# Two score buffers from pair 2 on, upper parts on ScalarE and remainders a unit later, in a hybrid attention layer on Trainium2

## The chip, the cores and the metric

The kernel runs on one core of one Trainium2 chip. The metric is the device time of one execution in microseconds, as the median of several runs. The engines are TensorE (PE; PEld is its weight load), VectorE (DVE), ScalarE (ACT), GpSimd (POOL) and SyncE (SP), whose queue issues nearly all transfers. Each engine works through its own instructions in order; semaphores order the engines among each other.

## The reference

One layer on 1024 tokens of width 1024, batch 1. The input is normalised, scaled and shifted, and projected to two groups of 8 heads of 64 columns: forgetting attention (a softmax with a bias from cumulated forget gates) and stick-breaking attention. Each head's output is gated by a SiLU, all are projected back, and a weighted residual is normalised again.

```python
u = _layer_norm(x) * (1.0 + scale) + shift
fq, fk, fv, fg, ff, sq, sk, sv, sg = _split_columns(u @ w_in)
f_cum = cumsum(log_sigmoid(ff + b_f))
# forgetting block: softmax over causal keys
s = q @ k.T * HEAD_DIM ** -0.5 + (f_q[:, None] - f_k[None, :])
fox = softmax(where(causal, s, -inf)) @ v
# stick-breaking block
z = q @ k.T * HEAD_DIM ** -0.5
later = reversed_cumsum(log_sigmoid(-z)) - log_sigmoid(-z)
sb = where(strict, exp(log_sigmoid(z) + later), 0.0) @ v
y = concat(fox * silu(fg), sb * silu(sg)) @ w_out
out = layer_norm(ALPHA * x + gate * y) * ln_g + ln_b
```

## The kernel before

The 16 heads are 8 pairs: pairs 0 to 3 are stick-breaking, 4 to 7 forgetting. A unit (p, h, i) is one head of one pair and one block of 128 queries against its (i + 1) * 128 causal keys, so there are 128 units. The list `units` (line 1193) goes pair by pair. In pairs 1 to 3 a head's blocks go upwards, in 4 to 6 downwards.

Matrix products are made of an upper and a lower part (`hi`, `lo`) of each operand, three products for a projection. The projections of later pairs (`gen_m` for queries, keys and gates, `gen_v` for values, `gen_split_out` for the output weights) are cut into steps and run as fillers between the units: the loop at line 1249 calls `scores_turn(k)`, `weights_turn(k)` and `fill(...)`, and `FILL` (line 1165) says how many steps a pair gets. TensorE's order is the program's; that of the other engines and of SP's queue is made by a scheduler from the dependencies, with `after(...)` to hold an instruction behind others.

What a unit does (`att_scores`, line 565):

- TensorE writes the scores to `S` (L578, L579), a tile of two PSUM banks with one buffer (line 75). The lower part of the query comes from `qz`, which ScalarE casts ahead (L525).
- In pairs 4 to 7 VectorE adds the forget bias and takes the minimum (L586); ScalarE makes the exponential and its sum (L591); VectorE makes the reciprocal and its scale (L592, L593) and adds the causal mask for the next unit (L563). POOL writes the upper float16 part of the weights (L596) and VectorE the remainder (L598) to a `room`.
- In pairs 0 to 3 ScalarE makes two sigmoids (L605, L607), VectorE a running product (L613, L617) and POOL the weights `be` (L619). From pair 2 on ScalarE writes the upper part (L626) and VectorE the remainder (L627) in the same unit.
- In pairs 0 and 1 the weights are turned by TensorE into a `T` bank (L643, two buffers) and copied by ScalarE and VectorE (L645, L646). From pair 2 on SP's queue turns them with a transposing transfer from `room` to `pt` (L551). A pair of blocks then multiplies the values (`att_pv`, L661), `LAG_CROSSED` = 4 units after the scores; ScalarE and VectorE add the two halves (L687, L688), POOL multiplies by the gate (L693), and the result goes to DRAM (L701).

Values of pairs 2 to 7 are float16 with a scale from the weights' norms. `squares` (L395) makes them from each group's split weights when that group's turn comes, on VectorE, and `range_of_v` (L398 to L408) follows before the first value tile can be evacuated. Output weights are loaded, multiplied by the gate vector, split by POOL and stored to `wo_dr` (L1019, L1020); `load_wo` brings them back in pair 7, when the tiles of `u` come free. `fetch_w` loads each weight piece to one of two staging tiles (L127), from which POOL makes the upper and lower part (L131, L132) in a ring of five.

```python
    def s_tile(name):
        return ps.tile([P, 2, 512], F32, tag="S", bufs=1, name=name)
...
            scaled[:] = [*scaled[-3:], nc.gpsimd.tensor_scalar(hi, ab, l, 1.0, op0=ALU.mult, op1=ALU.mult)]
            lows[:] = [*lows[-2:],
                       nc.vector.scalar_tensor_tensor(lo, ab, l, hi, op0=ALU.mult, op1=ALU.subtract)]
            cross(u, two)
```

Of the kernel before, what the change touches and what calls it, by code (L numbers as in the profile page):

```python
# [31 lines left out]
def tile_hybrid_layer(  # L32
# [333 lines left out]
    def range_of_u():  # L366
# [17 lines left out]
        top = t_tile("u_top")[:, 0:1]  # L384
        nc.tensor.matmul(top, ones[0:1, :].to_broadcast([1, P]), rng[0:1, 3:4], start=True, stop=True)
        nc.vector.tensor_scalar(rng[:, 4:5], top, 1.0e-30, None, op0=ALU.max)
        nc.vector.reciprocal(rng[:, 4:5], rng[:, 4:5])

    def squares(g, quarters):
        n = 528 if g == 1 else 512  # L390
        fr = rng[:, 5:9]
        for h, (hi, lo) in enumerate(quarters):
            hf = hi.bitcast(F32)[:, :n]
            sq = v_two[g].rearrange("p i t c -> p (i t c)").bitcast(BF16)[:, -n:]
            nc.vector.tensor_tensor_reduce(out=sq, in0=hf, in1=hf, op0=ALU.mult, op1=ALU.add, scale=1.0,  # L395
                                           scalar=0.0, accum_out=fr[:, h:h + 1])

    def range_of_v(g):  # L398
        fp = t_tile(f"v_range_{g}")[:, :4]
        nc.tensor.matmul(fp, ones.to_broadcast([P, P]), rng[:, 5:9], start=True, stop=True)  # L400
        up, down = (rng[:, c:c + 1] for c in (7 + 2 * g, 8 + 2 * g))
        nc.vector.tensor_reduce(out=up, in_=fp, op=ALU.add, axis=mybir.AxisListType.X)
# [124 lines left out]
    room, room_at, unsent = [], [0], []  # L527

    def two_parts(u):

        n = 2 * (u[2] + 1) * P
        if not room or u == ROOMS[len(room)]:
            room.append(sb.tile([P, 4 * SEQ], F16, tag="v", bufs=3, name=f"room_{len(room)}"))
            room_at[0] = 0
        if room_at[0] + n > 4 * SEQ:
            room_at[0] = 0
        two = room[-1][:, room_at[0]:room_at[0] + n]
        room_at[0] += n
        t4 = two.rearrange("p (b x c) -> p b x c", x=2, c=P)
        return two, t4[:, :, 0, :], t4[:, :, 1, :]  # L540
# [24 lines left out]
    def att_scores(u, following):  # L565
# [15 lines left out]
        if p >= 4:  # L581
# [3 lines left out]
            with after(*lows[:1]):  # L585
                nc.vector.tensor_tensor_reduce(out=v3(a), in0=S[:, :ns, :w], in1=v3(f),  # L586
                                               op0=ALU.add, op1=ALU.min, scale=-1.0, scalar=BIG,
                                               accum_out=nm)
# [7 lines left out]
            scaled[:] = [*scaled[-3:], nc.gpsimd.tensor_scalar(hi, ab, l, 1.0, op0=ALU.mult, op1=ALU.mult)]  # L596
            lows[:] = [*lows[-2:],
                       nc.vector.scalar_tensor_tensor(lo, ab, l, hi, op0=ALU.mult, op1=ALU.subtract)]  # L598
            cross(u, two)
        else:  # L600
# [22 lines left out]
            else:  # L623
                two, hi, lo = two_parts(u)
                bb = be[:, :ke].rearrange("p (b c) -> p b c", c=P)
                nc.scalar.activation(hi, bb, AF.Copy, scale=UP)  # L626
# [52 lines left out]
    def att_sum(acc, p, h, j):  # L679
# [20 lines left out]
        else:  # L700
            nc.sync.dma_start(y_dr[p, r, qs], yt[r, :])  # L701
# [630 lines left out]
```

## Time and profile before

| what | value |
|---|---|
| median of 3 runs | 726.84 us (726.46 to 730.42) |
| the profiled execution | 728.52 us |
| its span | 726.8 us, 10992 instructions |
| PE busy | 657.2 us (90%) |
| PEld busy | 540.3 us (74%) |
| DVE busy | 520.0 us (72%) |
| POOL busy | 434.3 us (60%) |
| ACT busy | 344.9 us (47%) |
| mean granted clock of TensorE | 0.958 |
| transferred | 109.87 MB, mean 151 GB/s |
| transposing transfers | 96, median 3.5 us to landing |

Busy time is an average over stages with different limits, so the tables by stage matter more. PEclk is the clock that TensorE was granted, 1.00 being full. A row of waits reads: engine, line, waited for; total us, times, longest us. A row of groups reads: line, engine, operation, tile written from tiles read, count; busy us, mean ns of one; idle time before them by releaser.

### The profile page before, as it was taken

The page shows a single profiled execution, that of the slowest core. Times are in us where ns is not written, and L with a number is a line of the kernel's source. Part 1 is how long each engine was busy: PE and PEld are TensorE (multiplying, and loading weights), DVE is VectorE, ACT ScalarE, POOL GpSimd, SP SyncE. Part 2 cuts the span into 40 slices and gives each one's busy share as a digit, 9 for nine tenths or more (in the row PEclk, how much of TensorE's full clock was granted, in tenths as well). Part 3 has the DMA queues.
Part 4 walks back from the last instruction along what each step waited for, and adds up shares of the span by engine and source line. Part 5 has one row for each costly group of instructions (what it writes and reads, how often), then busy time and mean ns, then how long its engine had stood idle before and what let it go on. Part 6 is the DMA issues. An engine that isn't in the chain of part 4 may idle for free.

```text
span 726.8 us, 10992 instructions
## 1 busy us (share of the span) xinstructions
PE 657.2 (90%) x3530; PEld 540.3 (74%) x3530; DVE 520.0 (72%) x1013; ACT 344.9 (47%) x753; POOL 434.3 (60%) x537
## 2 busy tenths in 40 slices
PE   8999999999999978969799788959998995799996
PEld 5798897788987766869677566749976763588785
DVE  6788689888668779975767645766777864596545
ACT  5567377656576656764634333424344542221000
POOL 6550576656385847681676777868795442675611
PEclk9999999999999999998999998978999998899999
DMA  9983331112023455452769777666786799867211
GB/s 333 398 296 118 102 72 44 41 41 63 5 66 86 100 129 118 103 141 51 204 138 185 173 190 199 166 169 179 196 216 153 161 343 275 215 168 194 95 58 59
DMA packets 160138, 109.87 MB, mean 151 GB/s; under 512 B 118928, under 2 KB 133840, under 8 KB 160080
## 3 DMA queue, kind: packets, MB, share of 16 engines
q1 hardware_dynamic: 158496, 104.70, 53.6%
q10 hardware_dynamic: 1584, 4.47, 2.3%
q8 instruction: 28, 0.46, 0.3%
q14 instruction: 30, 0.25, 0.1%
HBM read 60.34 MB, written 16.29 MB: 105 GB/s over the span
## 4 chain that ended last, share of the span: by engine, by line
PE 54%; POOL 10%; DMA 10%; issue 9%; DVE 9%; ACT 5%; SPq 1%; POOLq 0%; ACTq 0%; DVEq 0%
PE m L318 4%; DMA pt<-room 4%; PE pv L661 4%; PE m L316 4%; PE m L317 4%; PE o L1060 4%; PE o L1061 4%; PE o L1062 4%; DMA wss<-in_w_ss_dram 3%; PE S L578 3%; PE v L428 3%; PE v L430 3%; PE v L429 3%; PE S L579 3%; PE pv L672 2%
## 5 line engine op out<-in xcount | busy, mean ns | idle before, releaser
L316 PE MATMUL m<-uh,whi 128*128 128x512 f32 x304 | 124.9, 411 | 4.6 <-POOL whi L131 4.2
L318 PE MATMUL m<-uh,wlo 128*128 128x512 f32 x304 | 123.2, 405 | 4.4 <-POOL wlo L132 4.4
L317 PE MATMUL m<-ul,whi 128*128 128x512 f32 x304 | 122.1, 402 | 0.0
L619 POOL TENSOR_TENSOR be<-be,kp 128x127 f32<-128x127 f32 (+3 forms) x64 | 83.5, 1305 | 40.6 <-DVE kp L617 25.1
L598 DVE SCALAR_TENSOR_TENSOR room<-a,l,room 128x1024 f16<-128x1024 f32 (+4 forms) x64 | 70.3, 1102 | 39.9 <-POOL room L596 39.3
L578 PE MATMUL S<-k,q 128*128 128x512 f32 (+5 forms) x192 | 71.6, 374 | 18.2 <-DVE nm L586 15.3
L591 ACT ACTIVATE a<-a,nm 128x1024 f32<-128x1024 f32 (+3 forms) x64 | 49.7, 777 | 73.7 <-DVE nm L586 59.6
L596 POOL TENSOR_SCALAR room<-a,l 128x1024 f16<-128x1024 f32 (+4 forms) x64 | 53.0, 830 | 47.2 <-DMA pt<-room 15.8
L661 PE MATMUL pv<-pt,v_g 128*128 128x256 f16 x480 | 62.7, 284 | 14.0 <-DMA pt<-room 10.8
L318 PEld LDWEIGHTS m<-uh,wlo 128*128 128x128 f32 x304 | 58.7, 193 | 20.1 <-POOL wlo L132 6.1
L661 PEld LDWEIGHTS <-v_g 128*128 128x128 f16 x480 | 46.6, 105 | 33.3 <-issue 14.7
L613 DVE TENSOR_TENSOR_SCAN kp<-kp,floor 128x128 f32<-128x128 f32 (+3 forms) x64 | 58.6, 915 | 17.1 <-ACT kp L605 16.6
L316 PEld LDWEIGHTS m<-uh,whi 128*128 128x128 f32 x304 | 58.6, 193 | 16.2 <-POOL whi L131 5.5
L693 POOL TENSOR_TENSOR ty<-ty,sg 64x256 f32<-64x256 f32 x64 | 50.0, 782 | 29.1 <-DVE ty L688 19.4
L317 PEld LDWEIGHTS m<-ul,whi 128*128 128x128 f32 x304 | 58.5, 192 | 10.3
L579 PE MATMUL S<-kl,qz 128*128 128x512 f32 (+5 forms) x192 | 66.1, 346 | 0.0
L428 PE MATMUL v<-whi_v,uh 128*128 128x256 f32 (+1 forms) x192 | 57.3, 299 | 9.3 <-ACT room L626 5.4
L525 ACT CAST qz<-q 64x128 fp32r<-64x128 f32 x128 | 37.2, 295 | 51.4 <-PE S L579 50.0
L430 PE MATMUL v<-wlo_v,uh 128*128 128x256 f32 (+1 forms) x192 | 56.7, 295 | 4.0 <-POOL wlo_v L132 4.0
L578 PEld LDWEIGHTS S<-k,q 128*128 128x128 f32 x192 | 36.9, 192 | 31.2 <-DVE nm L586 21.8
L586 DVE CUSTOM_DVE_ANT_0 a<-S,fb 128x1024 f32<-128x1024 f32 (+3 forms) x64 | 48.2, 752 | 15.6 <-PE S L579 14.8
L605 ACT ACTIVATE kp<-S 128x384 f32<-128x384 f32 (+4 forms) x96 | 43.7, 491 | 32.8 <-PE S L579 31.5
(325 smaller groups left out, 1660.5 us busy)
## 6 DMA issues: line engine op xcount, KB each, us to landing
raw<-in_w_qkg_dram SPq DMA_DIRECT2D x38, 256.0 KB, 2.9
wss<-in_w_ss_dram SPq DMA_DIRECT2D x14, 512.0 KB, 8.3
x<-in_x_dram SPq DMA_DIRECT2D x8, 512.0 KB, 6.5
k<-k SPq DMA_DIRECT2D x32, 128.0 KB, 2.3
wg<-in_w_gate_dram SPq DMA_DIRECT2D x8, 512.0 KB, 4.8
raw_o<-in_w_out_dram SPq DMA_DIRECT2D x16, 256.0 KB, 3.1
fb<-f_dr ACTq DMA_DIRECT2D x8, 512.0 KB, 4.4
wo_dr<-whi_o SPq DMA_DIRECT2D x16, 256.0 KB, 2.4
```

What stands on the lines that cost most here:

```text
L316: nc.tensor.matmul(acc, hi[:, c], u_hi[kt][:, s], start=(kt == 0), stop=False)
L317: nc.tensor.matmul(acc, hi[:, c], u_lo[kt][:, s], start=False, stop=False)
L318: nc.tensor.matmul(acc, lo[:, c], u_hi[kt][:, s], start=False, stop=(kt == NB - 1))
L428: nc.tensor.matmul(acc[:, :n], u_hi[kt][:, ts_], hi[:, s], start=(kt == 0), stop=False)
L430: nc.tensor.matmul(acc[:, :n], u_hi[kt][:, ts_], lo[:, s], start=False, stop=(kt == NB - 1))
L578: nc.tensor.matmul(S[:, s, :w], qst[p][h][:, qs], kst[p][h][:, ks], start=True, stop=False)
L579: nc.tensor.matmul(S[:, s, :w], z, klo[p][:, ks], start=False, stop=True)
L596: scaled[:] = [*scaled[-3:], nc.gpsimd.tensor_scalar(hi, ab, l, 1.0, op0=ALU.mult, op1=ALU.mult)]
L598: nc.vector.scalar_tensor_tensor(lo, ab, l, hi, op0=ALU.mult, op1=ALU.subtract)]
L613: last_dve = nc.vector.tensor_tensor_scan(rv, rv, floor[:, :ke - lo], initial=0.0, op0=ALU.mult, op1=ALU.max)
L619: nc.gpsimd.tensor_tensor(be[:, :ke - 1], be[:, :ke - 1], kp[:, 1:ke], op=ALU.mult)
L661: nc.tensor.matmul(acc[:, q0:256], vt[p][:, kb, h * P:(h + 1) * P], pt[:, 2 * kb + x_, q0:], start=(kb == 0 and x_ == 0), stop=(kb == last ...
```

## The change

- From pair 2 on there are two score tiles, tags S and T. The two `T` banks, which only the first two pairs and the start use, are now one tile of two halves taken in turn, and scores alternate between it and S. The two small products of the forget rows use a score tile too, and so does the last piece of the output projection.
- In the forgetting pairs ScalarE writes the upper part instead of POOL. The remainder and the transfer of a unit are made in the next unit (`owed`, `pay`): after that unit's reduction, or in pairs 2 and 3 after its sigmoids and running product, where the upper part is moved too.
- Parts and turned weights have rooms of their own (`homes`): five fixed tiles, of which each block pair has its own stretch, while parts take the least recently used stretch. `LAG_CROSSED` is 5. Pairs 2 and 3 take their blocks from the large to the small.
- Stores of gated results and output weights are kept in a list and issued on SP's queue after a later unit's transfer.
- The norms of all value weights come from extra loads of the raw weights in pair 0, twelve loads and twelve squares, in place of `squares` and `range_of_v` in each group's turn.
- The last normalisation's gain and bias go to tiles of the query pool.

```diff
-        return ps.tile([P, 512], F32, tag="T", bufs=2, name=name)
-
-    def s_tile(name):
-        return ps.tile([P, 2, 512], F32, tag="S", bufs=1, name=name)
+        if not t_pair:
+            t_pair.append(ps.tile([P, 2, 512], F32, tag="T", bufs=1, name="t_pair"))
+        t_turn[0] += 1
+        return t_pair[0][:, t_turn[0] % 2, :]
+
+    def s_tile(name, one_of=1):
+        s_turn[0] += one_of - 1
+        return ps.tile([P, 2, 512], F32, tag="ST"[s_turn[0] % 2], bufs=1, name=name)
...
+        for g in range(1, 4):
+            n = 528 if g == 1 else 512
+            for h in range(4):
+                raw = raw_tile(f"n{g}_{h}")[:, :n]
+                nc.sync.dma_start(raw, w_vf[h] if g == 1 else w_v[g - 1, h])
+                at = 4 * g - 4 + h
+                nc.vector.tensor_tensor_reduce(out=raw, in0=raw, in1=raw, op0=ALU.mult, op1=ALU.add, scale=1.0,
+                                               scalar=0.0, accum_out=fr[:, at:at + 1])
+                for _ in range(NORM_SPACE):
+                    yield
...
+        two = place(parts_at, ((3, 0, 16), (2, 8, 16)), u[2] + 1)
+        return two.rearrange("p b (x c) -> p b x c", x=2)
...
+    def pay(*last):
+        while owed:
+            owed.pop(0)(*last)
+
+    def send(k):
+        while stores and stores[0][0] < k:
+            with after(*sent):
+                nc.sync.dma_start(*stores.pop(0)[1:])
...
-        S = s_tile(f"S_{p}_{h}_{i}")
+        S = s_tile(f"S_{p}_{h}_{i}", 1 if k_of[u] < 16 * FIRST_CROSSED + LAG else 2)
...
+            pay(reduced)
...
-            scaled[:] = [*scaled[-3:], nc.gpsimd.tensor_scalar(hi, ab, l, 1.0, op0=ALU.mult, op1=ALU.mult)]
-            lows[:] = [*lows[-2:],
-                       nc.vector.scalar_tensor_tensor(lo, ab, l, hi, op0=ALU.mult, op1=ALU.subtract)]
-            cross(u, two)
+            scaled[:] = [*scaled[-3:], nc.scalar.activation(hi, ab, AF.Copy, scale=l)]
+
+            def rest(last):
+                with after(last):
+                    lows[:] = [nc.vector.scalar_tensor_tensor(lo, ab, l, hi, op0=ALU.mult, op1=ALU.subtract)]
+                cross(u, two)
+            owed.append(rest)
...
-            nc.sync.dma_start(y_dr[p, r, qs], yt[r, :])
+            if p < FIRST_CROSSED:
+                nc.sync.dma_start(y_dr[p, r, qs], yt[r, :])
+            else:
+                stores.append((now[0], y_dr[p, r, qs], yt[r, :]))
...
-    LAG_CROSSED = 4
-    ROOMS = ((FIRST_CROSSED, 0, 0), (6, 0, 7), None)
+    LAG_CROSSED = 5
...
+            return [(p, h, i + d) for h in range(2) for i in (6, 4, 2, 0) for d in range(2)]
```

VectorE's queue in pair 5, head 0, before: `a_0_5` to `a_0_2` are the units of query blocks 5 to 2, `room` holds the parts. The reduction (L586) has two outputs, the second a row of its own, left out here.

```order
L586 ISA a_0_5_4836,nm_0_5_4837<-S_0_5_4831,fb_4315 128x768
...
L598 SCALAR_TENSOR_TENSOR room_2504<-a_0_6_4780,l_0_6_4782,room_2504 128x7x128
...
L598 SCALAR_TENSOR_TENSOR room_2504<-a_0_5_4836,l_0_5_4838,room_2504 128x6x128
L586 ISA a_0_4_4870,nm_0_4_4871<-S_0_4_4865,fb_4315 128x640
...
L586 ISA a_0_3_4929,nm_0_3_4930<-S_0_3_4926,fb_4315 128x512
...
L586 ISA a_0_2_4961,nm_0_2_4962<-S_0_2_4958,fb_4315 128x384
...
L598 SCALAR_TENSOR_TENSOR room_2504<-a_0_4_4870,l_0_4_4872,room_2504 128x5x128
```

The same place after the change, where `home` holds the parts, L610 is the reduction and L626 the remainder:

```order
L610 ISA a_0_6_4709,nm_0_6_4710<-S_0_6_4704,fb_4248 128x896
...
L626 SCALAR_TENSOR_TENSOR home_2529<-a_0_7_4660,l_0_7_4662,home_2529 128x8x128
...
L617 RECIPROCAL l_0_6_4711<-l_0_6_4711 128x1
...
L610 ISA a_0_5_4750,nm_0_5_4751<-S_0_5_4745,fb_4248 128x768
...
L626 SCALAR_TENSOR_TENSOR home_2529<-a_0_6_4709,l_0_6_4711,home_2529 128x7x128
...
L610 ISA a_0_4_4798,nm_0_4_4799<-S_0_4_4793,fb_4248 128x640
...
L626 SCALAR_TENSOR_TENSOR home_2619<-a_0_5_4750,l_0_5_4752,home_2619 128x6x128
```

A remainder now stands behind the reduction of the following unit, one to one; before, two remainders could follow each other, ahead of a reduction or behind several.

SP's queue between pairs 4 and 5, before: `raw` is a weight piece loaded to a staging tile, `whi_o` and `wlo_o` are split output weights, `ty` a gated result.

```order
L551 DMA_TRANSPOSE pt_1_1_4566<-room_2504 128x6x128
L1019 DMA wo_dr<-whi_o_0_4603 128x512
L1019 DMA wo_dr<-whi_o_1_4700 128x512
L701 DMA y_dr<-ty_1_3_4629 64x256
L1020 DMA wo_dr<-wlo_o_0_4604 128x512
L127 DMA raw_0_0_4730<-in_w_qkg_dram 128x512
L1020 DMA wo_dr<-wlo_o_1_4701 128x512
L127 DMA raw_0_1_4736<-in_w_qkg_dram 128x512
L551 DMA_TRANSPOSE pt_1_0_4656<-room_2504 128x4x128
```

And after, where L563 is the transposing transfer, L575 a store from the list and L135 a weight load:

```order
L563 DMA_TRANSPOSE home_2622<-home_2619 128x4x128
L575 DMA y_dr<-ty_1_3_4592 64x256
L575 DMA wo_dr<-wlo_o_0_4536 128x512
L135 DMA raw_0_0_4643<-in_w_qkg_dram 128x512
L575 DMA wo_dr<-whi_o_1_4631 128x512
L575 DMA wo_dr<-wlo_o_1_4632 128x512
L135 DMA raw_0_1_4649<-in_w_qkg_dram 128x512
L563 DMA_TRANSPOSE home_2622<-home_2619 128x2x128
L135 DMA raw_o_0_4731<-in_w_out_dram 128x512
L135 DMA raw_1_0_4824<-in_w_qkg_dram 128x512
L135 DMA raw_1_1_4830<-in_w_qkg_dram 128x512
L135 DMA raw_o_1_4836<-in_w_out_dram 128x512
```

The stores now stand right behind a transfer, and four weight loads stand ahead of the first transfer of pair 5.

VectorE's queue in pair 0 after the change: L389 is a square of raw weights `n`, L682 the remainder of weights that TensorE turned, L642 a running product, L727 a sum of two halves. Before, the rows between the squares stood there without them.

```order
L389 ISA n_3_940,modc<-n_3_940 128x528
...
L389 ISA n_0_952,modc<-n_0_952 128x512
...
L682 TENSOR_TENSOR pt_0_1_0_1029<-t_pair,pt_0_1_0_1029 128x3x128
L642 SCALAR_TENSOR_TENSOR kp_1_0_1041<-kp_1_0_1041,floor 128x128
...
L727 TENSOR_TENSOR ty_0_0_1051<-pv_0_0_1035,ty_0_0_1051 64x256
L389 ISA n_1_985,modc<-n_1_985 128x512
```

Five squares stand ahead of the running product of unit (1, 0) of pair 0, its fifth unit, and the twelfth stands ahead of that of unit (1, 3), its eighth.

More of the change, by code (lines that the diff above doesn't have):

```diff
@@ L383, in range_of_u @@
         yield
[L384 to L402, printed above, removed]
+        ps_r = t_tile("ranges")
+        nc.tensor.matmul(ps_r[:, 0:1], ones[0:1, :].to_broadcast([1, P]), rng[0:1, 3:4], start=True, stop=True)
+        nc.tensor.matmul(ps_r[:, 4:16], ones.to_broadcast([P, P]), fr, start=True, stop=True)
+        top = rng[:, 4:5]
+        nc.vector.tensor_scalar(top, ps_r[:, 0:1], 1.0e-30, None, op0=ALU.max)
+        nc.vector.reciprocal(top, top)
+        up, down = rng[:, 5:8], rng[:, 8:11]
+        nc.vector.tensor_reduce(out=up, in_=ps_r[:, 4:16].rearrange("p (g h) -> p g h", h=4), op=ALU.add,
+                                axis=mybir.AxisListType.X)
         nc.vector.tensor_scalar(up, up, 1.0e-30, None, op0=ALU.max)
-        nc.gpsimd.tensor_tensor(up, up, mhalf, op=ALU.pow)
-        nc.gpsimd.tensor_tensor(up, up, rng[:, 4:5], op=ALU.mult)
-        nc.vector.tensor_scalar(up, up, 900.0, None, op0=ALU.mult)
+        nc.gpsimd.tensor_tensor(up, up, mhalf.to_broadcast([P, 3]), op=ALU.pow)
+        nc.gpsimd.tensor_scalar(up, up, top, 900.0, op0=ALU.mult, op1=ALU.mult)
         nc.vector.reciprocal(down, up)
         nc.vector.tensor_scalar(down, down, 1.0 / UP, None, op0=ALU.mult)
-        v_up[g], v_down[g] = up, down
+        for g in range(1, 4):
+            v_up[g], v_down[g] = up[:, g - 1:g], down[:, g - 1:g]
     rng = bss_sb.rearrange("p k i -> p (k i)")
@@ L525, in att_query, with home, place, last_use @@
         nc.scalar.copy(z[r, :], qst[p][h].bitcast(F32)[r, i * P:i * P + P])
-    room, room_at, unsent = [], [0], []
-    def two_parts(u):
[L531 to L540, printed above, removed]
+    homes, parts_at = {}, []
+    HOMES = ((1, 12), (2, 0), (1, 0), (0, 0))
+    LAST_HOMES = ((1, 12), (4, 8), (2, 0), (4, 0), (1, 0), (0, 0), (0, 0), (4, 0))
+    def home(n):
+        if n not in homes:
+            homes[n] = (pt_tile(f"home_{n}", F16, [P, 2 * NB, 256]) if n < 3 else
+                        sb.tile([P, 2 * NB, 256], F16, tag="v", bufs=3, name=f"home_{n}"))
+        return homes[n]
+    def place(taken, spaces, n):
+        def last_use(c):
+            return max((t for t, (m, a, b) in enumerate(taken) if m == c[0] and a < c[1] + n and c[1] < b), default=-1)
+        m, a = min(((m, a) for m, lo, hi in spaces for a in range(lo, hi - n + 1)), key=last_use)
+        taken.append((m, a, a + n))
+        return home(m)[:, a:a + n, :]
+    def two_parts(u):
+        two = place(parts_at, ((3, 0, 16), (2, 8, 16)), u[2] + 1)
+        return two.rearrange("p b (x c) -> p b x c", x=2)
     def cross(u, two):
@@ L623, in att_scores, with rest @@
             else:
-                two, hi, lo = two_parts(u)
                 bb = be[:, :ke].rearrange("p (b c) -> p b c", c=P)
-                nc.scalar.activation(hi, bb, AF.Copy, scale=UP)
-                lows[:] = [nc.vector.scalar_tensor_tensor(lo, bb, UP, hi, op0=ALU.mult, op1=ALU.subtract)]
-                cross(u, two)
+                def rest(last, act=None):
+                    two = two_parts(u)
+                    hi, lo = two[:, :, 0, :], two[:, :, 1, :]
+                    with after(*[act] if act else ()):
+                        nc.scalar.activation(hi, bb, AF.Copy, scale=UP)
+                    with after(last):
+                        lows[:] = [nc.vector.scalar_tensor_tensor(lo, bb, UP, hi, op0=ALU.mult, op1=ALU.subtract)]
+                    cross(u, two)
+                pay(last_dve, last_act)
+                owed.append(rest)
             return last_act, last_dve
@@ L649, in att_transpose @@
                 att_pv(*between.pop(0))
-    y_last, summed = [], []
+    y_last, summed, now = [], [], [0]
     def att_pv(p, h, j):
@@ L705, in chain, with beside @@
             yield from g
-    def beside(main, side):
+    def beside(main, *sides):
         for x_ in main:
-            next(side, None)
+            for side in sides:
+                next(side, None)
             yield
-        for _ in side:
-            pass
+        for side in sides:
+            for _ in side:
+                pass
     START = ((0, 0), (0, 1), (0, 2), (1, 0), (1, 1))
@@ L1193, in tile_hybrid_layer @@
     units = [u for p in range(NPAIR) for u in order(p)]
+    k_of = {u: k for k, u in enumerate(units)}
     want = [0.0]
@@ L1213, in weights_turn @@
     def weights_turn(k):
+        now[0] = k
+        if k >= len(units):
+            pay(*lows)
+        while ready and k not in due:
+            att_pv(*ready.pop(0))
         for u in due.get(k, ()):
@@ L1245, in scores_turn @@
             p, h, i = units[k]
-            if 4 <= p < NPAIR - 1 and i == 0:
+            if 4 <= p < NPAIR - 1 and units[k + 1][:2] != (p, h):
                 load_fb(2 * (p - 4) + h + 2)
```

59 lines of the change are left out of this document (29 added, 30 removed).

## The prediction

> **What bounds the kernel now.** I read the busy time of each engine by stage first. The unit scores give the stages: pair 0 from 79 us, pair 2 from 213, pair 4 from 357, pair 5 from 437, pair 6 from 522, pair 7 from 583, output projection from 660.
>
> ```profile
> core 0: us, PE busy (x) PEld busy (x) DVE busy (x) ACT busy (x) POOL busy (x), PEclk, DMA share, GB/s
> 79.00:138.00 59.00, 57.12 (x336) 48.95 (x335) 48.38 (x82) 41.73 (x101) 44.37 (x59) 1.00 0.22 56
> 213.00:281.00 68.00, 62.95 (x306) 49.81 (x306) 52.03 (x64) 46.94 (x99) 44.14 (x57) 0.97 0.43 100
> 281.00:357.00 76.00, 66.54 (x423) 58.73 (x423) 58.30 (x90) 47.00 (x100) 47.86 (x58) 0.96 0.53 125
> 357.00:437.00 80.00, 68.68 (x324) 52.32 (x323) 50.99 (x117) 30.36 (x68) 54.22 (x58) 0.91 0.76 175
> 437.00:522.00 85.00, 72.22 (x424) 62.01 (x423) 56.37 (x142) 31.18 (x74) 64.17 (x67) 0.88 0.67 181
> 522.00:583.00 61.00, 55.00 (x284) 42.73 (x283) 45.85 (x116) 27.71 (x66) 40.67 (x43) 1.00 0.75 177
> 583.00:660.00 77.00, 63.90 (x298) 49.20 (x298) 53.01 (x125) 24.48 (x60) 41.68 (x50) 0.91 0.94 250
> 660.00:727.00 67.00, 59.70 (x286) 48.84 (x284) 34.53 (x58) 2.57 (x6) 25.30 (x33) 0.98 0.25 89
> ```
>
> TensorE is the bound: nearly always busy, except in pairs 2 to 7. There it is idle 14.5 us of 144 (pairs 2 and 3), 30.1 of 226 (pairs 4 to 6) and 13.1 of 77 (pair 7). Its granted clock falls there too: one minus the clock, times the stage, is 5.1, 17.4 and 6.9 us. So pairs 4 to 6 hold 226 - 30.1 - 17.4 = 178.5 us of TensorE work at full clock; this is the stage's lower end. Two neighbouring slices show how idleness and clock hang together:
>
> ```profile
> 415.00:420.00 5.00, 1.47 (x5) 0.59 (x4) 4.39 (x15) 3.66 (x8) 2.30 (x3) 1.00 1.07 240
> 420.00:425.00 5.00, 4.69 (x14) 3.65 (x14) 2.77 (x4) 0.17 (x1) 2.83 (x5) 0.66 0.85 188
> ```
>
> Then the waits of TensorE: total, times, longest. First pairs 2 and 3, then 4 to 6, then 7.
>
> ```profile
> PE v L428 <- ACT room L626: 5.4, 1, 5.4
> PE pv L661 <- DMA pt<-room: 3.8, 1, 3.8
> PE pv L661 <- DVE ty L688: 2.7, 1, 2.7
> PE S L578 <- ACT be L607: 2.0, 4, 0.9
> ```
> ```profile
> PE S L578 <- DVE nm L586: 12.6, 11, 3.4
> PE m L318 <- POOL wlo L132: 4.4, 4, 1.4
> PE m L316 <- POOL whi L131: 4.2, 3, 1.9
> PE v L430 <- POOL wlo_v L132: 4.0, 3, 1.8
> PE v L428 <- POOL whi_v L131: 3.7, 2, 3.4
> ```
> ```profile
> PE pv L661 <- DMA pt<-room: 6.9, 3, 4.6
> PE S L578 <- DVE nm L586: 2.7, 2, 2.4
> ```
>
> Last, who is late behind those, in pairs 4 to 6 (three rows) and on SP's queue in the whole run (two rows):
>
> ```profile
> DVE room L598 <- POOL room L596: 26.8, 27, 4.2
> POOL whi L131 <- DMA raw<-in_w_qkg_dram: 18.1, 6, 5.4
> POOL room L596 <- DVE l L593: 14.7, 10, 2.6
> ```
> ```profile
> SPq L701 <- POOL ty L693: 74.7, 26, 9.8
> SPq L127 <- POOL wlo L132: 20.9, 13, 5.8
> ```
>
> The reader sees a ring. POOL waits for VectorE's scale, VectorE for POOL's upper part, the one score buffer for VectorE's reduction behind that remainder, and SP's queue for POOL's results, with weight loads behind.
>
> **The change, part by part.** The profiled execution took 728.52 us (span 726.8), 1.7 above the median of 726.84; I sum from 728.5 and take 1.7 off at the end. The durations (ns) that the parts need:
>
> ```profile
> L578 PE MATMUL S<-k,q 128*128 128x512 f32 (+5 forms) x192 | 71.6, 374 | 18.2 <-DVE nm L586 15.3 <-ACT be L607 2.0 <-DMA k<-k 0.8
> L579 PE MATMUL S<-kl,qz 128*128 128x512 f32 (+5 forms) x192 | 66.1, 346 | 0.0
> L586 DVE CUSTOM_DVE_ANT_0 a<-S,fb 128x1024 f32<-128x1024 f32 (+3 forms) x64 | 48.2, 752 | 15.6 <-PE S L579 14.8
> L591 ACT ACTIVATE a<-a,nm 128x1024 f32<-128x1024 f32 (+3 forms) x64 | 49.7, 777 | 73.7 <-DVE nm L586 59.6 <-DVE l L593 6.2 <-POOL room L596 3.9
> L596 POOL TENSOR_SCALAR room<-a,l 128x1024 f16<-128x1024 f32 (+4 forms) x64 | 53.0, 830 | 47.2 <-DMA pt<-room 15.8 <-DVE l L593 14.7 <-DVE fb L563 5.9
> L598 DVE SCALAR_TENSOR_TENSOR room<-a,l,room 128x1024 f16<-128x1024 f32 (+4 forms) x64 | 70.3, 1102 | 39.9 <-POOL room L596 39.3
> L626 ACT ACTIVATE room<-be 128x128 f16<-128x128 f32 (+7 forms) x32 | 21.7, 683 | 20.5 <-POOL be L619 15.8 <-DMA pt<-room 2.8 <-POOL be L620 1.6
> L525 ACT CAST qz<-q 64x128 fp32r<-64x128 f32 x128 | 37.2, 295 | 51.4 <-PE S L579 50.0
> L563 DVE TENSOR_TENSOR fb<-fb,causal_ps 128x128 f32<-128x128 f32 x64 | 17.0, 283 | 0.9
> L592 DVE RECIPROCAL l<-l 128x1 f32<-128x1 f32 x64 | 10.1, 158 | 13.9 <-ACT a L591 13.1
> L593 DVE TENSOR_SCALAR l<-l 128x1 f32<-128x1 f32 x64 | 9.7, 152 | 1.7
> L395 DVE CUSTOM_DVE_ANT_0 v_g<-whi_v x12: 691/878/1765, 134.2 to 488.7; 128x512 bf16<-128x512 f32 x8, 128x528 bf16<-128x528 f32 x4
> ```
>
> *Pair 0: the value weights' norms, early.* Twelve more loads go through the two staging tiles, ahead of the loads of this pair's gate projection on SP's queue, and all twelve squares stand ahead of the running product of the pair's eighth unit on VectorE. At the median of L395 that is 12 x 0.878 = 10.5 us on an engine busy 48.4 of 59: 58.9, so no room is left, and the turned-weight remainders that TensorE's transposes wait for queue behind the squares. At 0.691 it is 8.3 (56.7 of 59, nothing lost); at 1.765 it is 21.2 (69.6, 10.6 lost). I take +6, nearer the middle, since an engine with in-order waits does not fill up.
>
> [...]
>
> *Pairs 2 and 3.* Scores wait no more for the one buffer (2.0), and the upper part stands behind the next unit's sigmoids, so ScalarE does not sit in front of POOL's product; the value scale is ready long before, which takes the 5.4. Of 3.8 + 2.7 for weights and sums not landed I take half, 3.2, as the product comes one unit later but so does the remainder. The forget rows hold a score buffer for some units: +1. Half of the clock's 5.1: 2.5. Sum -12; ends 0 (every wait is replaced) and -18.
>
> *Pairs 4 to 6.* A score needs the reduction of two units back, and the remainder now follows the next reduction instead of waiting ahead of it: the 12.6 go. POOL loses 48 x 0.830 = 39.8 us of its 159.1 and with it the waits for scale and room; SP's stores stand behind a transfer, when their data are long made, so raw weights load earlier: half of the 16.3 us of weight waits, 8. The clock follows the idleness: of 17.4 I take 8, as the drops sit at the weight waits that stay. A unit's transfer is issued one unit later and its product too, so the slack between them stays. ScalarE gains 48 x 0.683 = 32.8 us on top of 89.3, which fits. Sum -28, the stage at 198. What is late next: the transfers, whose shares make 0.76 x 80 + 0.67 x 85 + 0.75 x 61 = 163.6 us, 83% of 198; and VectorE, 153.2 us, 77%. Ends: -47 (the 178.5 above), and -8, if only the score waits go and a third of those comes back.
>
> *Pair 7.* The transfers fill 0.94 x 77 = 72.4 us of it, and none is removed; they bound the gain at 4.6 unless some move ahead. Of 6.9 and 2.7 us of waits I take -4; ends -10 and +3.
>
> *Nothing* for the start, which uses the same two banks in the same turn, and for the output projection from 660 on, which TensorE fills either way; the loads of the last normalisation's gain and bias only land in other tiles.
>
> Sum: 728.5 + 6 - 12 - 28 - 4 = 690.5; less 1.7: **689 us**.
>
> **The rivals.** *The transfers decide.* Pairs 4 to 6 cannot get above their best share, 0.76: 163.6 / 0.76 = 215, so -11; pair 7 gains nothing, pairs 2 and 3 gain 6: 728.5 + 6 - 11 - 6 - 1.7 = 716. For it: pair 7 stands still at 0.94. Against: slices of one or more show that the queue can be fuller.
>
> *Everything is fed.* Pairs 4 to 6 at 185 (-41), pairs 2 and 3 -18, pair 7 -8, pair 0 nothing: 660. For it: no single wait left would be long. [...]
>
> *Slower: ScalarE takes turns with VectorE.* The upper part now waits on ScalarE for VectorE's scale, and queued behind it is the query cast (L525) that a later score needs. If that ties each score to the unit before, a unit costs the whole chain: 1.5 x (0.374 + 0.346) for the score, 0.752, 0.777, 0.158 + 0.152, 0.683, 1.102, 0.283 and 0.295: 5.28 us, against 226 / 48 = 4.71 now. 48 units make 253, 27 more: 728.5 + 27 + 6 - 1.7 = 760. It decides once the chain exceeds 4.71. Against: two query tiles for each head, and the remainder covers the exponential.
>
> **How the numbers follow.** Forecast 0.65, transfers 0.17, everything fed 0.08, slower 0.08, and 0.02 for gains that pair 0 and pair 7 give back. All ends at once would span 652 to 730; 666 to 715 leaves out "everything fed", "slower" and the tops of the others. A measurement of this kernel tells some 0.5%, 3.6 us, from no change: faster 0.65 + 0.08 + 0.13, same 0.04 of the transfers' case and 0.02, slower 0.08.
>
> **What would show it.** Right: waits of scores for the reduction near nothing in pairs 4 to 6; the stage near 198 us with a clock of 0.95 or more and a transfer share above 0.8; POOL's busy time down by 53 and ScalarE's up by 44; pair 0 longer by some 6 us with VectorE above 90%. Wrong: ScalarE's upper part with long waits for the scale and scores behind the query cast; a pair 7 that grows by what the others gain; or product waits for turned weights in every pair.

## The result: slower, 752.6 us against 728.2

The changed kernel takes 752.6 us (median of four runs, 751.29 to 756.92) against 728.19 us of the kernel before in the same measurement; the ratio is 1.0344, with a 95% interval of 1.0287 to 1.04. Forecast were 689 us, in a range of 666 to 715. The profiled execution after took 751.29 us, its span 749.5, at a mean granted clock of 0.951 (before: 728.52, 726.8 and 0.958).

The stages, each from the first score of a pair to that of the next, in us:

| stage | before | after | change | forecast |
|---|---|---|---|---|
| start | 79.5 | 107.9 | +28.4 | 0 |
| pair 0 | 59.6 | 82.8 | +23.2 | +6 |
| pair 1 | 73.5 | 84.5 | +11.0 | 0 |
| pairs 2 and 3 | 141.3 | 129.2 | -12.1 | -12 |
| pairs 4 to 6 | 227.3 | 203.6 | -23.8 | -28 |
| pair 7 and output projection | 145.5 | 141.5 | -4.0 | -4 |

The changes are taken before rounding. From pair 2 on the forecast nearly holds: it is missed by 4 us, all of them in pairs 4 to 6. The rest of the error lies ahead of pair 2, where 62.6 us were lost and 6 expected. First the start and pair 1 of the kernel before, then the stages of the changed one up to the end of pair 6 (columns as in the first view above):

```profile
0.00:79.00 79.00, 77.00 (x394) 61.18 (x395) 61.59 (x115) 47.84 (x77) 30.99 (x59) 1.00 0.78 280
...
138.00:213.00 75.00, 74.09 (x468) 66.58 (x467) 59.00 (x111) 45.04 (x106) 40.94 (x58) 1.00 0.16 37
```
```profile
0.00:108.00 108.00, 87.39 (x398) 67.42 (x398) 62.43 (x116) 47.88 (x77) 30.86 (x59) 0.92 0.58 205
108.00:191.00 83.00, 65.30 (x345) 54.15 (x344) 59.52 (x109) 42.88 (x101) 49.95 (x62) 0.92 0.27 79
191.00:275.00 84.00, 74.48 (x453) 65.13 (x451) 52.89 (x97) 45.30 (x104) 41.57 (x56) 0.98 0.14 38
275.00:344.00 69.00, 63.00 (x317) 51.18 (x318) 56.28 (x65) 47.98 (x100) 44.16 (x53) 0.98 0.52 103
344.00:404.00 60.00, 60.00 (x404) 53.77 (x402) 49.48 (x72) 44.52 (x95) 43.97 (x56) 1.00 0.61 132
404.00:473.00 69.00, 64.60 (x327) 51.71 (x326) 44.61 (x118) 42.48 (x86) 45.12 (x42) 0.98 0.85 206
473.00:552.00 79.00, 67.99 (x416) 58.78 (x415) 50.86 (x125) 41.77 (x87) 48.66 (x47) 0.91 0.78 185
552.00:608.00 56.00, 53.94 (x287) 43.45 (x287) 43.10 (x119) 40.07 (x84) 30.97 (x31) 1.00 0.88 203
```

Read the start: VectorE and ScalarE have nearly the same busy time as before (62.43 and 61.59, 47.88 and 47.84), so no work was added. TensorE stands idle for 20.6 us of it where it was 2.0, and its clock falls from 1.00 to 0.92, which takes another 0.08 x 108 = 8.6 us. That makes 27 of the 28.4. The waits of the changed kernel in the start (first four rows), then in pairs 0 and 1:

```profile
ACT uh L275 <- PE t_pair L268: 22.5, 12, 5.8
DVE ul L288 <- ACT t_pair L276: 21.0, 11, 5.3
...
PE t_pair L814 <- DVE ul L288: 12.8, 6, 3.3
...
PE t_pair L268 <- DVE ul L288: 4.9, 3, 2.2
```
```profile
ACT pt L681 <- PE t_pair L679: 43.1, 34, 2.5
DVE pt L682 <- ACT pt L681: 24.5, 25, 1.8
...
PE t_pair L679 <- DVE pt L682: 18.7, 12, 3.4
```

TensorE's longest waits name t_pair, the one tile of two halves in which the change put the two small buffers, and end with VectorE's read of it: 12.8 + 4.9 = 17.7 us in the start and 18.7 in pairs 0 and 1. In the kernel before, such waits come to nothing in the start and to 1.0 us in pairs 0 and 1. The row with L814 shows the fault best: the start's query sums go into one half, the transposed input lies in the other, and the matmul into the first waits for VectorE's read of the second. In time, a stretch of the changed kernel (the rows that touch t_pair, pair 0), then one of the kernel before:

```profile
150.05 0.59 ACT L681 CAST pt<-t_pair 128x512 fp32r<-128x512 f32 x1 [1.28 <-PE t_pair L679]
150.67 0.69 DVE L682 TENSOR_TENSOR pt<-t_pair,pt 128x512 fp32r<-128x512 f32 x1 [0.47 <-ACT pt L681]
...
151.42 0.33 PE L679 MATMUL t_pair<-ident,be 128*128 128x128 f32 x1 [0.58 <-DVE pt L682]
151.78 0.27 ACT L681 CAST pt<-t_pair 128x128 fp32r<-128x128 f32 x1 [1.14 <-PE t_pair L679]
```
```profile
121.17 0.49 PE L643 MATMUL T<-ident,be 128*128 128x128 f32 x3
121.70 0.48 ACT L645 CAST pt<-T 128x384 fp32r<-128x384 f32 x1 [1.03 <-PE T L643]
122.61 1.15 DVE L646 TENSOR_TENSOR pt<-T,pt 128x512 fp32r<-128x512 f32 x2
```

Before, the second turn was transposed (121.17) and cast (121.70) ahead of the remainders of both turns (122.61, x2). After, a turn's remainder ends at 151.36 and only then does the next turn's transpose begin, at 151.42, though it writes the other half.

The program's own list of waits says it too. Of its 48 turns of transposes, 46 start with a wait for VectorE in the changed kernel, 28 in the kernel before; and in all 46 the VectorE instruction waited for is one that reads the other half, not the half about to be written. The same turn (second of unit 6, head 0, pair 0), first before, then after:

```
L643 MATMUL T_0_6_1_1409<-ident,be_0_6_1325 128x128 [waits PE_49]
L679 MATMUL t_pair<-ident,be_0_6_1338 128x128 [waits DVE_49]
```

In pairs 4 to 6, the waits of TensorE after:

```profile
PE m L324 <- POOL whi L139: 7.0, 3, 4.2
PE v L434 <- POOL whi_v L139: 3.8, 1, 3.8
PE m L326 <- POOL wlo L140: 3.0, 3, 1.4
...
PE v L436 <- POOL wlo_v L140: 0.8, 2, 0.5
```

No score waits for a reduction any more (12.6 us before). The weight waits, these four, stand at 14.6 us, where they were 16.3.

### The profile page after: what moved, and what is told of

It reads as the page before. It is cut to its first block, busy times and chain, and to the rows that moved or that the text cites. A ratio compares the mean times of both kernels' runs of the same rounds, so it can differ in the third digit from the quotient of the medians.

```text
span 749.5 us, 10970 instructions
## 1 busy us (share of the span) xinstructions
PE 660.3 (88%) x3526; PEld 544.0 (73%) x3526; DVE 507.9 (68%) x1002; ACT 391.7 (52%) x817; POOL 388.2 (52%) x469
## 4 chain that ended last, share of the span: by engine, by line
PE 59%; DMA 10%; DVE 10%; POOL 8%; issue 6%; ACT 5%; SPq 1%; POOLq 0%; ACTq 0%; DVEq 0%
PE m L324 6%; PE m L326 6%; PE m L325 6%; PE pv L697 5%; PE o L1101 4%; PE o L1103 4%; PE o L1102 4%; PE S L602 3%; PE S L603 3%; DMA home<-home 3%; PE v L434 3%; PE v L436 3%; PE v L435 3%; PE t_pair L679 2%; DMA raw<-in_w_qkg_dram 2%
## 5 line engine op out<-in xcount | busy, mean ns | idle before, releaser
L648 POOL TENSOR_TENSOR be<-be,kp 128x127 f32<-128x127 f32 (+3 forms) x64 | 90.2, 1410 | 42.3 <-DVE kp L646 22.5
L729 POOL TENSOR_TENSOR ty<-ty,sg 64x256 f32<-64x256 f32 x64 | 53.1, 830 | 65.2 <-DVE ty L724 49.0
L642 DVE TENSOR_TENSOR_SCAN kp<-kp,floor 128x128 f32<-128x128 f32 (+3 forms) x64 | 58.6, 915 | 22.9 <-ACT kp L634 22.3
L626 DVE SCALAR_TENSOR_TENSOR home<-a,l,home 128x1024 f16<-128x1024 f32 (+3 forms) x64 | 64.0, 1000 | 13.2 <-ACT home L622 12.6
L610 DVE CUSTOM_DVE_ANT_0 a<-S,fb 128x1024 f32<-128x1024 f32 (+3 forms) x64 | 48.1, 752 | 32.5 <-PE S L603 32.2
L603 PE MATMUL S<-kl,qz 128*128 128x512 f32 (+5 forms) x192 | 67.6, 354 | 0.0
L622 ACT ACTIVATE home<-a,l 128x1024 f16<-128x1024 f32 (+3 forms) x64 | 49.2, 773 | 35.3 <-DVE l L618 17.8
L616 ACT ACTIVATE a<-a,nm 128x1024 f32<-128x1024 f32 (+3 forms) x64 | 49.7, 776 | 26.2 <-DVE nm L610 23.2
L697 PE MATMUL pv<-home,v_g 128*128 128x256 f16 x480 | 57.8, 269 | 1.0 <-DVE ty L724 0.7
L697 PEld LDWEIGHTS <-v_g 128*128 128x128 f16 x480 | 44.4, 100 | 17.5 <-issue 10.4
L435 PE MATMUL v<-whi_v,ul 128*128 128x256 f32 (+1 forms) x192 | 55.2, 287 | 0.0
L140 POOL TENSOR_TENSOR wlo<-raw,whi 128x512 fp32r<-128x512 f32 x38 | 52.7, 1389 | 1.7
```

The source lines that it names most:

```text
L435: nc.tensor.matmul(acc[:, :n], u_lo[kt][:, ts_], hi[:, s], start=False, stop=False)
L603: nc.tensor.matmul(S[:, s, :w], z, klo[p][:, ks], start=False, stop=True)
L626: lows[:] = [nc.vector.scalar_tensor_tensor(lo, ab, l, hi, op0=ALU.mult, op1=ALU.subtract)]
L642: last_dve = nc.vector.tensor_tensor_scan(rv, rv, floor[:, :ke - lo], initial=0.0, op0=ALU.mult, op1=ALU.max)
L648: nc.gpsimd.tensor_tensor(be[:, :ke - 1], be[:, :ke - 1], kp[:, 1:ke], op=ALU.mult)
L697: nc.tensor.matmul(acc[:, q0:256], vt[p][:, kb, h * P:(h + 1) * P], pt[:, 2 * kb + x_, q0:], start=(kb == 0 and x_ == 0), stop=(kb == last ...
```

## The experiments

Theory A: the two halves of t_pair take turns as if they were one buffer, and this alone turns the gain into a loss. Theory B: it costs the start only, and pair 0's loss is the twelve squares at their far end. After these two were told apart, the other runs priced parts of the change. The time of a run is its median; the stages come from its profiled execution. Ratios are to the kernel before in the same measurement. The rooms (`homes`), `LAG_CROSSED` of 5 and the new order of pairs 2 and 3 have no run of their own.

**Two tiles (e1_two_tiles).**

```
-            t_pair.append(ps.tile([P, 2, 512], F32, tag="T", bufs=1, name="t_pair"))
-        return t_pair[0][:, t_turn[0] % 2, :]
+        return tps.tile([P, 512], F32, tag="T", bufs=2, name=name)     # tps: a pool of its own
...
+        if s_turn[0] and len(s_pools) < 2:
+            t_stack.close()                                            # its banks come free
+            s_pools.append(ctx.enter_context(tc.tile_pool(name="s2", bufs=1, space=bass.MemoryType.PSUM)))
```

> The changed kernel with the one tile of two halves (t_pair) taken back to two tiles of one bank each, as before the change; from pair 2 on a new pool takes over their two banks for the second score buffer. Everything else of the change stays. Theory A, the halves of one tile take turns as if they were one: against the kernel before, the start had lost 28 us, pair 0 23 and pair 1 11; the tile is to blame for all but the 6 us of the norms in pair 0, so the start is back at 80 us, pair 0 at 65, pair 1 at 74, and the time is 752.6 - 28 - 17 - 11 = 697 us (690 to 703). Theory B, the tile costs the start alone and pair 0 is longer by the twelve squares at their far end (12 x 1.765 = 21.2 us): 752.6 - 28 = 725 us, down to 714 if pair 1 comes back too, with pair 0 still near 80 us and VectorE's squares in its path.

694.46 us; the ratio to before is 0.9532 (0.9469 to 0.9594). Its start, pair 0 and pair 1:

```profile
0.00:80.00 80.00, 77.52 (x399) 61.73 (x400) 62.59 (x116) 47.77 (x77) 30.94 (x59) 1.00 0.77 276
80.00:150.50 70.50, 62.67 (x344) 54.10 (x343) 57.56 (x108) 42.65 (x102) 47.15 (x61) 0.93 0.34 93
150.50:222.50 72.00, 72.00 (x455) 64.95 (x455) 52.77 (x99) 44.71 (x105) 40.37 (x56) 1.00 0.15 38
```

The start is back at 79.7 us and pair 1 at 72.0; pair 0 is at 70.5. Theory A holds, B falls; only A's split was off, since pair 0 keeps 10.9 us of its loss where A gave 6 to the norms. This version beats both kernels: it takes 58 us less than the changed one, and all that was edited is where two buffers are declared.

**The one tile alone (e2_pair_only).** The kernel before, with only this:

```
     def t_tile(name):
-        return ps.tile([P, 512], F32, tag="T", bufs=2, name=name)
+        if not t_pair:
+            t_pair.append(ps.tile([P, 2, 512], F32, tag="T", bufs=1, name="t_pair"))
+        t_turn[0] += 1
+        return t_pair[0][:, t_turn[0] % 2, :]
```

> The kernel before with one edit: t_pair, one tile of two halves, in place of the two one-bank buffers. Theory A: the start grows by 28 us, pair 0 by 17, pair 1 by 11, the pairs after that by nothing as they have no turned weights: 728.2 + 56 = 784 us (775 to 795). Theory B: only the start grows, 728.2 + 28 = 756 us, up to 767 with pair 1. If the halves are free of each other, 728.

789.85 us, ratio 1.0845 (1.0783 to 1.0907), 60.2 us above the 729.66 of before in the same measurement. In the profiled execution (793.37 us, the longest of the four) the start grows by 30.2 us, pair 0 by 15.3, pair 1 by 12.2; pairs 4 to 6 grow by 7.1, where t_pair holds only sums for a value scale; that part stays open. With the run above, this settles it from both sides.

**The norms left out (e3_no_norms), loads alone (e11_loads_alone), squares alone (e12_squares_alone).** All start from e1_two_tiles; the sums of squares are a constant in the first two.

```
 # e3: both out; e11: only the second; e12: only the first, squaring a resident tile
-                nc.sync.dma_start(raw, w_vf[h] if g == 1 else w_v[g - 1, h])
-                nc.vector.tensor_tensor_reduce(out=raw, in0=raw, in1=raw, ..., accum_out=fr[:, at:at + 1])
+        nc.gpsimd.memset(fr, 0.5)                        # e3, e11
```

> As the kernel with two one-bank tiles (e1_two_tiles), with the twelve early norm loads and squares left out: the sums of squares are set to a constant, so the scale of the values is not the computed one. Prices the early norms. Theory A: pair 0 shorter by my 6 us, the rest the same, 691 us if the other gives 697. Theory B: shorter by 21 us or more, 693 to 704 if the other gives 714 to 725. Bounds of the price as stated before: 0 and 10.6 us.

> As e1_two_tiles (694.5 us, pair 0 70.5), with the twelve norm loads and without their squares: the sums of squares are a constant, so the value scale is not the computed one. Theory A, the squares fill VectorE: pair 0 back near 60 us, 684 to 686. Rival, the loads' turn through the two staging tiles and SP's queue makes the weight splits late: pair 0 keeps 66 us or more, 690 to 694.

> As e1_two_tiles, with the twelve squares and without their loads: they square a tile that is there (the modulated input's), so the value scale is not the computed one. Theory A: pair 0 stays within 2 us of its 70.5, 692 to 696. Rival, VectorE's standing still for the landing (4.7 us in the two-tile run) is the price, and the squares fit without it: pair 0 at 62 us or less, 685 to 688.

684.05, 690.07 and 698.66 us (ratios 0.9396, 0.9405 and 0.9546). Pair 0 in each, in the same order:

```profile
80.00:138.50 58.50, 57.11 (x340) 49.28 (x339) 48.73 (x83) 41.72 (x100) 45.72 (x61) 1.00 0.22 58
```
```profile
80.00:144.50 64.50, 60.13 (x341) 52.31 (x340) 48.02 (x83) 42.25 (x101) 45.05 (x61) 0.95 0.38 102
```
```profile
80.00:149.00 69.00, 61.20 (x343) 52.24 (x342) 59.84 (x107) 42.58 (x102) 48.60 (x61) 0.95 0.19 49
```

Pair 0 takes 59.1 us without norms, 64.9 with the loads, 69.1 with the squares, 70.5 with both. The squares are the larger price (10.0 alone), as A said, but the loads cost 5.8 alone, which A had not. Alone they cost more than both together (15.8 against 11.4); the squares of the last run are the longer ones, 0.934 us at the median against 0.689 beside the loads. In the whole time the squares alone can't be told from both. The early norms cost 11.4 us in pair 0, 10.4 in the time. The clock carries some of it: at 0.93 of 70.5 us it takes 4.9, where it was 1.00. TensorE's matmuls stand idle in that stage for 7.8 us with both and 1.4 without norms, and the longest wait with both is for VectorE:

```profile
PE gate L966 <- DVE gate L967: 2.8, 1, 2.8
```

So VectorE is late there, though at 57.56 busy of 70.5 us it isn't full.

**The norms where they were (e8_norms_back)**, on the kernel with one score buffer (below): the norm code of the kernel before put back.

```
-            ..., gen_gate(), gen_ranges()),
+            ..., chain([gen_gate(), range_of_u()])),
+            squares(g, quarters)                  # in gen_v, from the split weights
+                range_of_v(g)                     # in v_tile, at a group's first tile
```

> As e4_one_score_buffer (698.0 us), with the norms of the value weights computed as before the change, group by group from the split weights behind each group's loads, not early from loads of their own. Theory A: pair 0 gives back the 10.4 us that the run without the norms showed, and the squares hide later as they did before: 688 us. Rival: they cost in pairs 2 to 5 what pair 0 gains, since VectorE is on the path there too: 698.

703.66 us, ratio 0.9657 (0.9626 to 0.9689), above both times that were expected. Pair 0 gives back its 10.4 us (70.0 to 59.6), but pair 3 grows from 60.7 to 74.1. Pair 3 with norms back, with its longest wait, then with early norms:

```profile
279.20:353.30 74.10, 63.53 (x406) 56.22 (x404) 57.30 (x85) 44.63 (x95) 46.59 (x56) 0.95 0.51 111
```
```profile
PE v L429 <- DVE v_g L442: 6.8, 1, 6.8
```
```profile
288.20:348.90 60.70, 60.48 (x405) 54.10 (x404) 50.08 (x72) 44.54 (x95) 44.31 (x54) 1.00 0.61 135
```

So nearly all of the gain of pairs 2 and 3 hangs on the norms' move: without it they take 140.7 us (before: 141.3), with it TensorE is busy 60.48 of pair 3's 60.70 us at full clock. Whether it is the earlier scale or the VectorE work that leaves pair 3 (57.30 us busy against 50.08), the two runs don't tell apart. The rival was right in kind: norms cost where they stand. By the stages pair 0 is the cheaper place; the intervals of the two times just overlap.

**One score buffer (e4_one_score_buffer).** Two one-bank tiles to the end (the forget rows and the last output piece use them again), and `s_tile` always from the one tag.

```
-        return ps.tile([P, 2, 512], F32, tag="ST"[s_turn[0] % 2], bufs=1, name=name)
+        return ps.tile([P, 2, 512], F32, tag="S", bufs=1, name=name)
```

> The changed kernel with two one-bank tiles as in e1_two_tiles, kept to the end, and only one score buffer throughout; the upper parts on ScalarE, the later remainders, the rooms and the late stores stay. Prices the second score buffer. Theory A of my sum: the waits of scores for the reduction (12.6 us in pairs 4 to 6, 2.0 in pairs 2 and 3) come back, some 15 us above e1_two_tiles, so 712 if that gives 697. Rival: the remainder's later place already frees the one buffer in time, and the second buffer is worth 0 to 4 us.

698.04 us, ratio 0.9602 (0.954 to 0.9665), which overlaps that of e1_two_tiles. Pairs 4 to 6 take 200.1 us with one buffer and 202.5 with two. The rival holds: the second score buffer, for which t_pair was made, brings nothing that these runs can tell, and without it no tile has to be joined.

**Upper part back on POOL (e5_upper_on_pool), remainder at once (e6_rest_at_once), stores at once (e7_stores_at_once).** The first and the last start from e1_two_tiles, the second from e4_one_score_buffer.

```
 # e5
-            scaled[:] = [*scaled[-3:], nc.scalar.activation(hi, ab, AF.Copy, scale=l)]
+            scaled[:] = [*scaled[-3:], nc.gpsimd.tensor_scalar(hi, ab, l, 1.0, op0=ALU.mult, op1=ALU.mult)]
 # e6: the remainder and cross(u, two) in place, not by owed.append(rest)
-            with after(*lows):
+            with after(*lows[:1]):
 # e7
-                stores.append((now[0], y_dr[p, r, qs], yt[r, :]))
+                nc.sync.dma_start(y_dr[p, r, qs], yt[r, :])        # and the two of wo_dr
```

> As e1_two_tiles (694.5 us), with the upper part of the forgetting units back on POOL; it still has a unit's time, since the remainder stays a unit later. Theory C, the gain of pairs 4 to 6 (227 to 202.5 us there) comes from taking 48 x 0.83 = 40 us off POOL: at least 16 of the 25 come back, so 710 us or more, with POOL's raw weights late again. Theory D, it comes from the remainder's new place, so that VectorE does not stand waiting for the upper part: at most 6 come back, 695 to 700.

> As e4_one_score_buffer (698.0 us), with the remainder of the forgetting units and their transposing transfer issued at once, as before the change, with the upper part on ScalarE. Theory C: ScalarE's upper part alone does it, 698 to 702. Theory D: the remainder is again ahead of the next reduction on VectorE, which waits for the scale and the upper part, and the one score buffer with it: 714 us or more, and TensorE's score waits for the reduction come back to some 12 us in pairs 4 to 6.

> As e1_two_tiles (694.5 us), with the stores of the sums and of the split output weights issued where they were before the change, not behind the next transfer. My sum counted on half of the 16.3 us of weight waits of pairs 4 to 6 from this and from POOL's relief: 700 to 703 if the stores do it. Rival: the queue's stores delay loads that have time; 694 to 697.

711.09 (ratio 0.9751, 0.9716 to 0.9786), 716.89 (0.9853, 0.9814 to 0.9891) and 702.53 us (0.9655, 0.9614 to 0.9695). Of e5, pairs 4 to 6 and the waits of TensorE there:

```profile
348.50:568.10 219.60, 192.75 (x1023) 156.79 (x1022) 148.69 (x360) 89.90 (x209) 162.00 (x166) 0.93 0.74 183
```
```profile
PE m L324 <- POOL whi L139: 10.1, 5, 3.2
PE m L326 <- POOL wlo L140: 5.2, 6, 1.4
PE v L434 <- POOL whi_v L139: 4.8, 1, 4.8
...
PE v L436 <- POOL wlo_v L140: 2.8, 3, 2.0
```

Theory C holds for e5: with the upper part on POOL, 17.0 of the 25 us come back, and the weight waits are 22.9 us (13.8 in e1_two_tiles). Of e6, a wait in pairs 4 to 6 (where it is 8.4 us longer than e4) and one in pair 7:

```profile
PE S L594 <- DVE nm L602: 2.8, 3, 1.2
```
```profile
PE pv L687 <- DMA home<-home: 23.7, 1, 23.7
```

Theory D's mechanism falls: even with one buffer and the remainder ahead of the reduction, scores wait 2.8 us for it, not 12. Its price comes out all the same, 18.9 us, by another way: 8.4 in pairs 4 to 6 and 13 in pair 7 and after, where one product waits 23.7 us for its turned weights. Why that transfer comes so late was not settled. Of e7, pairs 4 to 6 take 212.5 us (10 more than e1), and the product waits appear:

```profile
PE pv L697 <- DMA home<-home: 4.6, 2, 2.5
```

The stores' place is worth 8 us, as the sum had allowed; yet not by the weight waits (13.8 us in e1_two_tiles, 14.6 here) but at least in part by products that wait for transfers. The three prices in pairs 4 to 6 (17.0, 8.4 and 10) add up to more than the gain of 25 there: they overlap.

**Norms beside pair 1's projections (e9_norms_in_pair_1) or on ScalarE (e10_norms_on_act)**, from e1_two_tiles.

```
 # e9
-        beside(..., gen_gate(), gen_ranges()), gen_m(2, 0), gen_m(2, 1), gen_v(1),
+        beside(..., gen_gate()), beside(chain([gen_m(2, 0), gen_m(2, 1)]), gen_ranges()), gen_v(1),
 # e10
+                nc.scalar.activation(raw, raw, AF.Square, accum_out=fr[:, at:at + 1])
```

> As e1_two_tiles (694.5 us), with the twelve norm loads and squares beside the projections of pair 1 in place of pair 0's. Theory A, the 10.4 us are the price of a full VectorE (57.6 busy of 70.5 in pair 0, against 52.7 of 71.9 in pair 1): pair 0 back to 59 us, pair 1 at 72 to 75, 684 to 688 us, and pair 3 keeps its 60 us, as the value scale is still early. Rival: the loads and squares cost wherever they stand, by their loads' turn on the queue: pair 1 grows by what pair 0 gains, 694.

> As e1_two_tiles (694.5 us), with the twelve squares in pair 0 on ScalarE (a Square with its sum) in place of VectorE; loads unchanged. Theory A: VectorE is what was full; ScalarE is busy 42.6 of 70.5 there, so pair 0 comes back to 60 to 63 us and the time to 684 to 689. Rival, the loads through the two staging tiles and SP's queue cost it: pair 0 stays near 70 us, 692 to 695.

698.35 us (0.9547, 0.9487 to 0.9607) and 692.09 us (0.9502, 0.9449 to 0.9556): neither can be told from e1_two_tiles. The first did not do what it was made for. Its squares still ran from 110.5 to 145.4 us, ahead of pair 1's first score at 149.1, since that pair's projections are taken up early; pair 0 took 69.7. In the second, pair 0 took 67.4 with VectorE busy 48.5: relief of VectorE alone gives 3 of the 11, as ScalarE now stands for the landing of the loads (5.9 us).

## Why the prediction was wrong, and where it was right

**The step that failed:** "*Nothing* for the start, which uses the same two banks in the same turn". The banks and the turn are the same, and the sentence is true of both. What it left out, and so put at nothing, is that the program's waits go by the tile here: with one tile for both halves, an instruction that writes one half waits for the reader of the other. (Why they do stays open.) Priced by taking it away, that is 28.2 us in the start, 12.3 in pair 0 and 12.5 in pair 1 (the changed kernel less e1_two_tiles, stage by stage), 53 of the 55 us of span between the two; priced by adding it, 60 us. None of the rivals held this wait. The rival that ended slower named ScalarE's turns with VectorE at 760 us; it came within 8 us of the time by luck, through a mechanism that isn't there, since pairs 4 to 6 became shorter. No run shows the 41 us that "everything is fed" took off pairs 4 to 6: with two tiles they are 24.8 us shorter, at a clock of 0.96. Two slips of the working changed little: the ends of its terms add up to 732 at the top (728.5 + 10.6 - 8 + 3 - 1.7), not 730, and TensorE doesn't fill the output projection, where it is idle for 7.3 of 67 us.

**Pair 0, +6.** With two tiles it is 70.5 us against 59.6: +10.9, just past the far end of the 0 to 10.6 that the squares were given, and not for the reason of that end. The squares are no longer than the nearer rows said (median 0.689 us, 9.8 us of VectorE in all, in e1_two_tiles). What the norms cost is TensorE's: 7.8 us in which it is idle, with 2.8 as the longest wait, for VectorE, and a clock of 0.93. The loads, which I costed at nothing, have a part in it (5.8 us of the stage alone). How far an engine with in-order waits fills up, by which I took 6, was my estimate; the sign that I gave, VectorE above 90%, did not come: it is busy 82% of the stage there, and 72% in the changed kernel.

**Pairs 2 and 3, -12.** Right in size (-12.1; -13.6 with two tiles), wrong in its parts. I put 5.4 us on the value scale and the rest on the score buffer, landings and the clock. Nearly all of it comes with the norms' move: with the norms back, pair 3 is back at 74.1 us.

**Pairs 4 to 6, -28.** It is -23.8, the stage at 203.6 us for 198. The score waits went, as said; but they go with one buffer too, and 2.8 us of them return with the remainder at once, so what removed them is the relief of the ring elsewhere. The whole stage, before and in e1_two_tiles:

```profile
354.00:581.30 227.30, 198.04 (x1038) 159.09 (x1039) 156.01 (x379) 90.71 (x211) 161.70 (x170) 0.92 0.72 178
```
```profile
350.00:552.50 202.50, 186.81 (x1022) 153.34 (x1021) 140.13 (x360) 123.81 (x257) 122.89 (x118) 0.96 0.82 197
```

TensorE's idle time fell by 13.6 us (29.3 to 15.7), and its busy time by 11.2, with the clock at 0.96 for 0.92. The 8 us on weight waits did not come (16.3 to 14.6): this is more than the miss.

**Pair 7, -4,** and the listed signs: the stage and the output projection are 4.0 us shorter; POOL lost 46 us of busy time (53 forecast), ScalarE gained 47 (44); the transfer share in pairs 4 to 6 is 0.83 and the clock 0.96. With the tile's wait taken away, the whole change gives 694.46 us, 5.5 above the forecast.

## What to carry to other kernels

Joining two buffers into one tile was here an edit of the waits (46 of 48 turns of transposes start with one for VectorE, 28 before), with banks and turns the same: list the waits of the changed program on the engines that write and read it, in every stage that uses the buffers, before pricing anything else; here the edit was made for pairs 2 to 7 and cost in the three stages before them. Price a moved step where it lands and where it leaves: the early norms cost 10 us in pair 0 and gave 13 in pair 3 (both by the run with the norms back).

## What the runs showed of the hardware

**Squares that started within a POOL instruction ended after it.** Pair 0 of e9_norms_in_pair_1, in time:

```profile
116.32 0.68 DVE L389 CUSTOM_DVE_ANT_0 n<-n 128x528 f32<-128x528 f32 x1
...
118.15 2.27 POOL L648 TENSOR_TENSOR be<-be,kp 128x895 f32<-128x895 f32 x1 [3.82 <-DVE kp L646]
...
119.28 1.71 DVE L389 CUSTOM_DVE_ANT_0 n<-n 128x528 f32<-128x528 f32 x1
...
121.02 0.69 DVE L682 TENSOR_TENSOR pt<-T,pt 128x512 fp32r<-128x512 f32 x1
...
121.86 0.63 PE L679 MATMUL T<-ident,be 128*128 128x128 f32 x4 [3.61 <-DVE pt L682]
```

A square of the same shape takes 0.68 us beside no POOL instruction and 1.71 when it starts within one; it ends 0.57 after POOL's product does (120.42). Behind it the turned-weight remainder is late, and TensorE stands for 3.61 us, of which the longer square can explain some 1 us. In the changed kernel three squares start within a POOL instruction that goes on for 0.8 us or more (at 115.25, 119.45 and 135.63): they take 1.43, 1.55 and 1.34 us, where the median is 0.68, and end 0.54 to 0.57 us after it. Across the twelve squares of e1_two_tiles the lengthening is small: 9.8 us of VectorE against 8.3 at the median.

**Behind a gap of 2.4 us the clock was 0.51.** The start of the changed kernel, cut around one gap:

```profile
38.00:41.60 3.60, 3.60 (x18) 2.64 (x16) 1.79 (x4) 0.40 (x1) 1.83 (x2) 1.00 1.03 391
41.60:44.10 2.50, 0.07 (x2) 0.04 (x1) 1.97 (x4) 1.56 (x3) 0.87 (x1) 1.00 1.05 419
44.10:44.60 0.50, 0.50 (x2) 0.45 (x3) 0.50 (x1) 0.00 (x0) 0.40 (x1) 1.00 1.06 434
44.60:48.00 3.40, 3.40 (x9) 2.64 (x8) 3.29 (x8) 0.10 (x1) 1.05 (x3) 0.51 0.44 177
```

TensorE was idle for 2.4 us, busy for 0.5, and then had 0.51 of its clock for 3.4 us. If that clock is put to the gap, this stall cost 2.4 + 0.49 x 3.4 = 4.1 us, an estimate from these slices. The longest gap of the start after the first matmul is 3.3 us, and the mean clock of the start 0.92. The two slices at 415 and 420 of the kernel before hold no single long gap: their idle time is three gaps of 0.8, 1.8 and 1.2 us with matmuls between, and the clock of the second slice is 0.66. What sets the clock was not measured.
